# Copied scan states stored as chunk, component, group, together with another order of y rows, outputs and transfers

## The chip, the cores and the metric

The kernel runs on one core of one Trainium2 chip. The metric is the time of one execution on the device, in microseconds, taken over several runs. Five engines work side by side, each through its own instructions in order: TensorE (PE, with its weight loads as PEld), VectorE (DVE), ScalarE (ACT), GpSimd (POOL) and SyncE (SP), which here only issues transfers. A tile scheduler fixes the order in which each engine's instructions stand.

## The reference, cut to what matters

Two sequences (1024 and 512 tokens, 1536 together) go through an attention layer and then through a state-space layer ("S5"). Only the second half of the program, the S5 layer, is changed:

```
u, gate = jnp.split(x @ w_in, 2, axis=-1)
...
bu = einsum('lgp,gnp->lgn', us, b_bar)              # 64 groups, 64 complex states each
_, h = lax.associative_scan(_ssm_combine, (a, bu))  # h[t] = lam * h[t-1] + bu[t], forward and backward
y = einsum('gpn,lgn->lgp', c, h).real + d * uf
y = jax.nn.gelu(y)
y = y * jax.nn.sigmoid(y @ w_glu + b_glu)
return (y * jax.nn.silu(gate)) @ w_out
```

## The kernel before, in words

Tokens are taken in chunks of eight: the 1536 tokens are 192 chunks, 128 of the long sequence and 64 of the short one. What a chunk does within itself is one product with a table `tt`; what it gets from earlier chunks comes through the states at the chunk borders. The scan over those border states runs on VectorE (`step`, L1242 to L1249). It has two halves of 32 groups each, `X[0]` (zone SA) and `X[1]` (zone SB), each stored as chunk, component (real or imaginary), group: 192 x 2 x 32 numbers in a partition, so that two chunks of one group lie 64 numbers apart. Partitions 0 to 63 hold the forward states, 64 to 127 the backward ones, whose chunks run the other way.

Sixteen output steps follow, `i` = 0 to 15, four groups each. `load_s(i)` (L1360) fetches three tiles over SP: `uc` (inputs), `tt` and `wo`. `states_out(i)` (L1371) copies the four groups of `X` into a small tile `st`, turned round in time for the backward half: three copies on ScalarE, L1375, L1376 and L1377, of 1536, 1024 and 512 numbers a partition. `outputs(i, st)` (L1380) makes for each group three products into one PSUM bank: `tt` with `uc` (L1391) and the two components of `wo` with `st` (L1392, L1393). Weights stay in the array; `uc` and `st` are the operands that stream through it, 192 columns each. These products are plain f32, and each is two MATMUL instructions in the trace. ScalarE applies Gelu (L1395), and after every second step eight transfers write a row block `Y[m]` of y to memory (L1399).

The first `N0` = 10 output steps are woven into the last gate passes. A gate pass (`gate`, L1338) multiplies x with the gate weights, which come through six slots of zone R (`load_wg`, L1324); each `mm3` there is three fp32r products (L89, L90, L91) of 512 columns. `between` says behind which of the 48 gate steps of the last six passes an output step stands. `advance` emits scan steps by a running account of microseconds.

After the gate passes comes the GLU: `load_y(m)` brings `Y[m]` back (1536 numbers a partition) and splits it into a rounded part and a rest, on GpSimd for m below 4 (L1440, L1442); `load_w(m)` brings 1/8 of `w_glu` in two halves (L1452) and splits them on ScalarE (L1453) and VectorE (L1454). The raw halves of `load_w(1)` lie in memory that x held (zone X1), so that they can be loaded only when the gate products are done with x. Six output steps, 10 to 15, are woven with the first GLU products (`early`). What is behind that, the rest of the GLU and the output projection, is the same in both kernels.

Of the kernel before, what the change touches and what calls it, by code (L numbers as in the profile page):

```python
# [20 lines left out]
NT = LP + LS  # L21
# [1168 lines left out]
def s5(k):  # L1190
# [59 lines left out]

    owed = [0.0]

# [5 lines left out]
    def advance(us):  # L1258


        owed[0] += us
        while owed[0] > 0 and any(todo.values()):
            steps = [(*h, todo[h].pop(0)) for h in todo if todo[h]]
            owed[0] -= 0.47 * len(steps) if len(steps) > 1 else 0.72
            if len(steps) == 1:
                steps = [(*steps[0], 0, 16), (*steps[0], 16, 32)]
            for f in zip(*[step(*x) for x in steps]):
                for g in f:
                    g()

# [56 lines left out]

    M0, N0 = 2, 10
    passes = [(m, (0, 1, 2)) for m in range(M0)] + [(m, (0,)) for m in range(M0, 8)] + [(m, (1, 2)) for m in range(M0, 8)]
# [8 lines left out]
    def gate(i):  # L1338
        m, cs = passes[i]
        acc = {c: ps_b() for c in cs}  # L1340
        for kt in range(8):
            if i < 2 and kt % 2 == 0:
                states_in(8 + 4 * i + kt // 2)
            if (i, kt) == (1, 6):
                begin(1)
            wg = w.pop((i, kt))
            for c in cs:
                mm3(nc, acc[c], (wg[:, 0, :], wg[:, 1, :]), xk(c, kt), kt == 0, kt == 7)
            fetch()
            advance(0.69 * len(cs) + (1.8 if i < 2 else 0))  # L1350
            if i >= 8 and (i - 8) * 8 + kt in between:
                between.pop((i - 8) * 8 + kt)()
        for c in cs:
            sg = k.rr.tile([128, 512], F32, "sg", 9, 11)
            nc.scalar.copy(sg, acc[c])
            nc.scalar.dma_start(k.SG2[m, :, c * 512:(c + 1) * 512], sg)
# [3 lines left out]
    def load_s(i):  # L1360
        reg, at = ((xa, 0), (xa, 16), (xb, 0))[i % 2 if i < N0 else (i - N0) % 3]
        tag = "%s%d" % ("b" if reg is xb else "a", at)
# [8 lines left out]
    def states_out(i):  # L1371
        reg, at = ((k.xn, 0), (xa, 25))[i % 2]
        st = reg.tile([128, 2, 4, 192], F32, "st", at)
        xv = X[i // 8][:, :, :, (i % 8) * 4:(i % 8) * 4 + 4].rearrange("p c r g -> p r g c")
        nc.scalar.copy(st[0:64], xv[0:64])  # L1375
        nc.scalar.copy(st[64:128, :, :, 0:128], xv[64:128, :, :, 127::-1])  # L1376
        nc.scalar.copy(st[64:128, :, :, 128:192], xv[64:128, :, :, 191:127:-1])  # L1377
        return st

    def outputs(i, st):  # L1380
# [31 lines left out]
    def first(i):  # L1412
        if i == 8:
            advance(1e3)
        outputs(i, states_out(i))
        advance(1.3)
        load(i + 2)

    n = (8 - M0) * 8
    between = {0: lambda: load(0), 3: lambda: load(1)}  # L1420
    for i in range(N0):
        between[6 + (n - 7) * i // max(N0 - 1, 1)] = lambda i=i: first(i)
    for i in range(8, 8 + 8 - M0):
# [4 lines left out]
    xb, xc = Region(k, "X1", (24, F32), (8, F32R)), Region(k, "X2", (32, F32R))  # L1428
    sy = Region(k, "SA", (48, F32R))
    yat = {m: (sy, 12 * m) for m in range(4)}  # L1430
    yat.update({4: (xc, 0), 5: (xc, 12)})
    gat = [(xc, 24), (xb, 24)]
    ys = [None] * 8

    def load_y(m):
        reg, at = yat[m]
        y = reg.tile([128, 2, NT], F32R, "y%d" % m, at)
        raw = bits(y[:, 1])
        nc.sync.dma_start(raw, k.Y[m])
        nc.gpsimd.tensor_scalar(y[:, 0], raw, 1.0, 0.0, op0=ALU.mult, op1=ALU.add)  # L1440

        (nc.gpsimd if m < 4 else nc.vector).tensor_sub(y[:, 1], raw, y[:, 0])  # L1442
        ys[m] = y

    def load_w(m):
        reg, at = gat[m % 3]
        w = reg.tile([128, 2, 8, 128], F32R, "glu", at)
        for h in range(2):
            reg, at = (xb, 22 if m < 3 else (16, 12)[m % 2] + 2 * h) if m else (k.xn, 6 + 2 * h)
            raw = reg.tile([128, 4, 128], F32, "graw%d" % at, at)  # L1450
            hs = slice(4 * h, 4 * h + 4)
            nc.sync.dma_start(raw, k.w_glu[m, :, hs])  # L1452
            nc.scalar.copy(w[:, 0, hs], raw)  # L1453
# [25 lines left out]

    load_y(0)  # L1480
    ws = [load_w(0), load_w(1)]
    load_y(1)
    load(N0 + 2)
    st = states_out(N0)
    big = [ps_s(), ps_s()]
    acc = [[big[i][:, 0:512], big[i][:, 512:1024], ps_b()] for i in range(2)]

    def early(kt):
        if 0 < kt < 5 or kt == 6:
            load_y(kt + 1)  # L1490
        for c in (2, 0, 1):
# [4 lines left out]
    for i in range(N0, 16):  # L1496
        cur = st
        if i < 15:
            st = states_out(i + 1)
        outputs(i, cur)  # L1500
        if i < 13:
            load(i + 3)
        while done < (0, 0, 3, 4, 5, 6)[i - N0]:
            early(done)
            done += 1
        if i == 13:
            x0 = Region(k, "X0", (16, F32R))
            yat[6] = (x0, 0)
            load_y(6)
    while done < 6:  # L1510
# [4 lines left out]
    so = Region(k, "SB", (48, F32R))  # L1515
    gat.append((so, 40))
    early(6)
    ws.append(load_w(2))
    part = [ps_b(), ps_b()]
# [168 lines left out]
```

## Time and profile before

| what | us |
|---|---|
| runs of the kernel before (3) | 1617.59, 1629.79, 1630.28 |
| their median | 1629.79 |
| the profiled execution | 1624.55 |
| its span from first to last instruction | 1622.8 |
| TensorE busy in the span | 1565.0 |
| mean granted TensorE clock | 0.991 |

The profiled execution is 5.2 us under the median and 7 us over the fastest run. Its 1.75 us outside the span are not touched by the change. "Busy" of TensorE counts a matmul from its start to the modelled end of its results, so that two matmuls that follow each other closely overlap; what one costs in a stream is the distance from start to start.

### The profile page before, as it was taken

The numbers are of one execution on the slowest core, as the hardware profiler recorded it, in microseconds if no ns is written. First come the engines' busy times: TensorE is split into PE (matmuls) and PEld (weight loads), VectorE is DVE, ScalarE is ACT, GpSimd is POOL, SyncE is SP. The second block draws the span as 40 slices with busy tenths as digits, with TensorE's granted clock in tenths as the row PEclk, the third lists the DMA queues.
The fourth block names the chain that finished last, engine by engine and source line by source line (L and its number), as shares of the span: only waits on it lengthen the run. The fifth ranks groups of instructions, "written<-read, shape, count | busy, mean of one in ns | idle before, by whom it ended". The sixth has DMA issues, their size and how long they took to land.

```text
span 1622.8 us, 23654 instructions
## 1 busy us (share of the span) xinstructions
PE 1565.0 (96%) x7948; PEld 1324.9 (82%) x7948; DVE 1104.4 (68%) x3077; ACT 633.2 (39%) x1056; POOL 322.7 (20%) x532
## 2 busy tenths in 40 slices
PE   8999999999999999999999999999899889999997
PEld 7997878788888788888888888888678768888886
DVE  5559992767676766888677742499599812565866
ACT  3544331444544445444410113416657367442000
POOL 6820000422223222343201000000000311233110
PEclk9999999999999999999999999999999989999999
DMA  5656566523122325533444427525678857565543
GB/s 194 186 157 207 165 234 219 161 78 92 56 84 86 115 87 182 181 98 103 156 132 127 131 74 192 155 46 157 205 234 245 272 148 229 189 212 162 178 139 88
DMA packets 205929, 249.67 MB, mean 154 GB/s; under 512 B 26608, under 2 KB 149104, under 8 KB 204784
## 3 DMA queue, kind: packets, MB, share of 16 engines
q1 hardware_dynamic: 197168, 232.36, 47.7%
q10 hardware_dynamic: 8640, 15.80, 2.6%
q8 instruction: 63, 1.03, 0.3%
q14 instruction: 58, 0.48, 0.1%
HBM read 155.89 MB, written 90.11 MB: 152 GB/s over the span
## 4 chain that ended last, share of the span: by engine, by line
PE 67%; DVE 12%; DMA 10%; ACT 5%; issue 2%; SPq 2%; POOL 1%; ACTq 0%; DVEq 0%; POOLq 0%
PE B L90 10%; PE B L89 10%; PE B L91 10%; PE S L89 8%; PE S L91 8%; PE S L90 8%; PE B L552 3%; DVE SA L1249 2%; DVE scan L1248 2%; PE S L1229 2%; PE S L518 2%; PE S L517 2%; DMA X<-SG 1%; DMA SA<-CH 1%; DMA X<-in_s_w_out 1%
## 5 line engine op out<-in xcount | busy, mean ns | idle before, releaser
L89 PE MATMUL B<-X,SB 128*128 128x512 f32 x392 | 155.3, 396 | 0.0
L90 PE MATMUL B<-X,SB 128*128 128x512 f32 x392 | 154.0, 393 | 0.0
L91 PE MATMUL B<-X,SB 128*128 128x512 f32 x392 | 153.9, 393 | 0.0
L537 POOL TENSOR_SCALAR SC<-SC,R 128x1024 f32<-128x1024 f32 (+1 forms) x96 | 99.7, 1039 | 209.9 <-DVE R L536 187.1
L554 ACT CAST X<-B 128x512 fp32r<-128x512 f32 x160 | 89.5, 591 | 128.3 <-PE B L552 127.7
L555 DVE TENSOR_TENSOR X<-B,X 128x512 fp32r<-128x512 f32 x160 | 105.7, 682 | 25.5 <-ACT X L554 25.2
L530 ACT ACTIVATE SC<-S,R 128x1024 f32<-128x1024 f32 (+1 forms) x96 | 93.9, 978 | 63.1 <-DVE R L527 58.2
L527 DVE TENSOR_REDUCE R<-S 128x1 f32<-128x1024 f32 (+1 forms) x96 | 99.1, 1038 | 21.9 <-PE S L518 21.6
L552 PE MATMUL B<-ident,SC 128*128 128x128 f32 x640 | 88.7, 272 | 2.0 <-POOL SC L537 2.0
L89 PE MATMUL B<-X,R 128*128 128x512 f32 x192 | 79.2, 413 | 10.7 <-DMA R<-WG 7.3
L552 PEld LDWEIGHTS B<-ident,SC 128*128 128x128 f32 x640 | 76.2, 140 | 16.2 <-POOL SC L537 2.7
L91 PEld LDWEIGHTS B<-X,SB 128*128 128x128 f32 x392 | 74.1, 189 | 15.3
L90 PEld LDWEIGHTS B<-X,SB 128*128 128x128 f32 x392 | 74.1, 189 | 14.7
L89 PEld LDWEIGHTS B<-X,SB 128*128 128x128 f32 x392 | 73.9, 189 | 14.6
L1249 DVE TENSOR_TENSOR SB<-SB,scan 128x32 f32<-128x32 f32 (+1 forms) x504 | 80.8, 213 | 0.5 <-DMA R<-WG 0.5
L1248 DVE TENSOR_TENSOR scan<-SB,lam 128x64 f32<-128x64 f32 (+1 forms) x252 | 64.9, 293 | 17.4 <-ACT SB L1237 17.4
L89 PE MATMUL S<-SA,X 128*128 128x384 f32 (+2 forms) x208 | 70.8, 345 | 5.9 <-POOL SA L96 5.4
L90 PE MATMUL B<-X,R 128*128 128x512 f32 x192 | 76.1, 396 | 0.0
L91 PE MATMUL B<-X,R 128*128 128x512 f32 x192 | 75.8, 395 | 0.0
L1249 DVE TENSOR_TENSOR SA<-SA,scan 128x32 f32<-128x32 f32 (+1 forms) x504 | 75.4, 200 | 0.0
L90 PE MATMUL S<-SA,X 128*128 128x384 f32 (+2 forms) x208 | 70.6, 341 | 0.4 <-DVE SA L97 0.4
L91 PE MATMUL S<-SA,X 128*128 128x384 f32 (+2 forms) x208 | 70.1, 339 | 0.4 <-DVE X L1454 0.4
(454 smaller groups left out, 4230.8 us busy)
## 6 DMA issues: line engine op xcount, KB each, us to landing
R<-WG SPq DMA_DIRECT2D x112, 128.0 KB, 3.5
R<-EU SPq DMA_DIRECT2D x52, 224.0 KB, 3.4
EU<-SA SPq DMA_DIRECT2D x16, 512.0 KB, 3.6
WO<-SA SPq DMA_DIRECT2D x8, 1024.0 KB, 5.3
WG<-X SPq DMA_DIRECT2D x16, 512.0 KB, 3.0
X<-WO SPq DMA_DIRECT2D x16, 512.0 KB, 5.9
SG<-SC ACTq DMA_DIRECT2D x24, 256.0 KB, 3.0
SC<-SG SPq DMA_DIRECT2D x24, 256.0 KB, 2.9
```

The costliest lines, as they stand in the source:

```text
L89: nc.tensor.matmul(ps, ah, bh, start=first, stop=False)
L90: nc.tensor.matmul(ps, ah, bl, start=False, stop=False)
L91: nc.tensor.matmul(ps, al, bh, start=False, stop=last)
L517: nc.tensor.matmul(S[:, cs], qs[:, q], self.kr[kc][0], start=False, stop=False)
L527: nc.vector.reduce_max(nm, self.S[:, :L], axis=AX.X, negate=True)
L530: nc.scalar.activation(P, self.S[:, :L], AF.Exp, bias=nm, accum_out=rsum)
L537: nc.gpsimd.tensor_scalar(P, P, rsum, 0.0, op0=ALU.mult, op1=ALU.add)
L552: nc.tensor.transpose(ps[:, t, :], P[:, (t0 + t) * 128:(t0 + t + 1) * 128], self.k.ident)
L554: nc.scalar.copy(a[:, :, qsl], ps)
L555: nc.vector.tensor_sub(b[:, :, qsl], ps, a[:, :, qsl])
L1248: return [lambda: nc.vector.tensor_mul(t, prev.unsqueeze(2).broadcast_to(sh), lam), lambda: nc.vector.tensor_add(cur, cur, t[:, 0]), lambd ...
L1249: lambda: nc.vector.tensor_add(cur, cur, t[:, 0]), lambda: nc.vector.tensor_add(cur, cur, t[:, 1])]
```

## The change

The code changes in five places.

- `states_out` stores `st` as chunk, component, group (192 x 2 x 4). A copy now reads and writes in the same order, in runs of four numbers, and the products L1398 and L1399 (L1392 and L1393 before) read `st` with a step of eight numbers from column to column. For steps 8 to 15 the forward copy goes to VectorE, held behind the scan's last instruction.
- `N0` is 8: eight output steps stand among the gate passes, and eight (half 1 of the scan) are woven with the GLU.
- The y rows 0 to 2 are fetched while the gate passes still run (`rows`), their rounding goes to ScalarE (`hi_y`) and the rest to VectorE behind the scan (`lo_y`); GpSimd keeps the rounding of rows 4 to 7.
- The slots and the order of the transfers of `load_s` change for the last steps, and some y and `w_glu` transfers are kept where they are written.
- The gate results of the first two passes lie in the zone of `st` instead of zone R.

```diff
-    M0, N0 = 2, 10
+    M0, N0 = 2, 8
...
-            sg = k.rr.tile([128, 512], F32, "sg", 9, 11)
+            sg = k.xn.tile([128, 512], F32, "sg", 0, 2, 4, 6) if i < 2 else k.rr.tile([128, 512], F32, "sg", 9, 11)
...
-        st = reg.tile([128, 2, 4, 192], F32, "st", at)
-        xv = X[i // 8][:, :, :, (i % 8) * 4:(i % 8) * 4 + 4].rearrange("p c r g -> p r g c")
-        nc.scalar.copy(st[0:64], xv[0:64])
-        nc.scalar.copy(st[64:128, :, :, 0:128], xv[64:128, :, :, 127::-1])
-        nc.scalar.copy(st[64:128, :, :, 128:192], xv[64:128, :, :, 191:127:-1])
+        st = reg.tile([128, 192, 2, 4], F32, "st", at)
+        xv = X[i // 8][:, :, :, (i % 8) * 4:(i % 8) * 4 + 4]
+        if i < N0:
+            nc.scalar.copy(st[0:64], xv[0:64])
+        else:
+            with k.tc.issue_after(last[0].ins):
+                nc.vector.tensor_copy(st[0:64], xv[0:64])
+        nc.scalar.copy(st[64:128, 0:128], xv[64:128, 127::-1])
+        nc.scalar.copy(st[64:128, 128:192], xv[64:128, 191:127:-1])
...
-                nc.tensor.matmul(o, wo[:, 0, g, :], st[:, 0, g, :], start=False, stop=False)
-                nc.tensor.matmul(o, wo[:, 1, g, :], st[:, 1, g, :], start=False, stop=True)
+                nc.tensor.matmul(o, wo[:, 0, g, :], st[:, :, 0, g], start=False, stop=False)
+                nc.tensor.matmul(o, wo[:, 1, g, :], st[:, :, 1, g], start=False, stop=True)
...
+    def fetch_y(m):
+        reg, at = yat[m]
+        ys[m] = reg.tile([128, 2, NT], F32R, "y%d" % m, at)
+        pin(nc.sync.dma_start(bits(ys[m][:, 1]), k.Y[m]))
+
+    def hi_y(m):
+
+        y = ys[m]
+        if m < 4:
+            pin(nc.scalar.copy(y[:, 0], bits(y[:, 1])))
+        else:
+            nc.gpsimd.tensor_scalar(y[:, 0], bits(y[:, 1]), 1.0, 0.0, op0=ALU.mult, op1=ALU.add)
+
+    def lo_y(m):
+        with k.tc.issue_after(last[0].ins):
+            nc.vector.tensor_sub(ys[m][:, 1], bits(ys[m][:, 1]), ys[m][:, 0])
...
-        between[6 + (n - 7) * i // max(N0 - 1, 1)] = lambda i=i: first(i)
+        between[6 + (n - 12) * i // (N0 - 1)] = lambda i=i: first(i)
+    between[n - 5] = rows
+    between[n - 1] = lambda: [hi_y(m) for m in range(3)]
...
-    load_y(0)
-    ws = [load_w(0), load_w(1)]
-    load_y(1)
+    st = states_out(N0)
+    ws = [load_w(0)]
     load(N0 + 2)
-    st = states_out(N0)
+    ws.append(load_w(1))
+    fetch_y(3)
...
+        if i < 11:
+            lo_y(i - 8)
+        elif i == 11:
+            hi_y(3)
+            lo_y(3)
+        elif i in (12, 14):
+            load_y(i // 2 - 2)
         outputs(i, cur)
-        if i < 13:
-            load(i + 3)
-        while done < (0, 0, 3, 4, 5, 6)[i - N0]:
+        for x in ((), (11,), (12, 13), (14,), (15,), (), (), ())[i - N0]:
+            load(x)
+        while done < (0, 0, 1, 2, 3, 3, 4, 4)[i - N0]:
             early(done)
             done += 1
```

TensorE at the end of the gate passes. The last gate products write a bank `B` from x (`X_91`) and zone R; the GLU products write the double bank `S` from y rows (`SA`) and the split `w_glu` of block 0 (`X_11904`, after `X_11864`) or 1 (after `X_11863`). Before:

```order
L91 MATMUL B<-X_91,R 128x512
L1391 MATMUL B<-X_10777 128x192 x2
L89 MATMUL S<-SA,X_11904 128x512
L90 MATMUL S<-SA,X_11904 128x512
L91 MATMUL S<-SA,X_11904 128x512
```

After:

```order
L91 MATMUL B<-X_91,R 128x512
L1397 MATMUL B<-X_10776 128x192 x2
L1397 MATMUL B<-X_10777 128x192 x2
L89 MATMUL S<-SA,X_11864 128x512
L89 MATMUL S<-SA,X_11863 128x512
L90 MATMUL S<-SA,X_11864 128x512
L91 MATMUL S<-SA,X_11864 128x512
L90 MATMUL S<-SA,X_11863 128x512
```

Before, 48 GLU products follow here and then the output steps 10 onward; after, 14 of them stand ahead of output step 8, and the third already needs the rest part of y row 0.

VectorE at the end of the scan (L1248 and L1249 on `SB`), with the split of the two halves of `load_w(1)` (`X_11903`, after `X_11863`). Before, the rest parts of y rows 0 to 3 are not in this list, since GpSimd makes them:

```order
L1249 TENSOR_TENSOR SB<-SB,scan_81 128x2x16 x3
L1454 TENSOR_TENSOR X_11903<-X_11902,X_11903 128x512
L1249 TENSOR_TENSOR SB<-SB,scan_81 128x2x16
L1248 TENSOR_TENSOR scan_81<-SB,lam 128x4x16 x2
L1249 TENSOR_TENSOR SB<-SB,scan_81 128x2x16 x4
L1442 TENSOR_TENSOR X_11904<-X_11904 128x1536
```

After, 18 scan instructions stand behind the second half, then the rest of y row 0 and the forward copies of steps 8 and 9:

```order
L1249 TENSOR_TENSOR SB<-SB,scan_81 128x2x16 x4
L1478 TENSOR_TENSOR X_11863<-X_11862,X_11863 128x512
L1248 TENSOR_TENSOR scan_81<-SB,lam 128x4x16 x2
L1249 TENSOR_TENSOR SB<-SB,scan_81 128x2x16 x4
L1248 TENSOR_TENSOR scan_81<-SB,lam 128x4x16 x2
L1249 TENSOR_TENSOR SB<-SB,scan_81 128x2x16 x4
L1248 TENSOR_TENSOR scan_81<-SB,lam 128x4x16 x2
L1249 TENSOR_TENSOR SB<-SB,scan_81 128x2x16 x4
L1442 TENSOR_TENSOR SA<-SA 128x1536
L1381 COPY XN<-SB 64x1536
L1381 COPY X_10777<-SB 64x1536
```

The end of the scan, and with it everything on VectorE behind it, stands in both kernels behind the split of `load_w(1)`.

SyncE at the same place, before (`X_11902` is the raw slot of `w_glu`, and the tiles of an output step where it reads EU, CH, WO):

```order
L1399 DMA Y<-X_10776 16x8x192 x8
L1324 DMA R<-WG 128x256 x4
L1439 DMA SA<-Y 128x1536
L1452 DMA X_11902<-in_w_glu 128x512
L1364 DMA X_11902<-EU 128x4x192
```

After:

```order
L1325 DMA R<-WG 128x256 x5
L1366 DMA X_10777<-EU 128x4x192
L1368 DMA X_10777<-CH 128x512
L1370 DMA X_10777<-WO 128x2x512
L1405 DMA Y<-X_10776 16x8x192 x8
L1366 DMA X_11862<-EU 128x4x192
L1368 DMA X_11862<-CH 128x512
L1370 DMA X_11862<-WO 128x2x512
L1476 DMA X_11862<-in_w_glu 128x512 x3
```

The last gate weights now go ahead of the eight y writes, and the first half of `load_w(1)` goes behind the three tiles of an output step instead of ahead of them.

## Rows read from the trace of the kernel before

**Rows 1.** The page, part 1: busy us, share, instructions of each engine.
```profile
PE 1565.0 (96%) x7948; PEld 1324.9 (82%) x7948; DVE 1104.4 (68%) x3077; ACT 633.2 (39%) x1056; POOL 322.7 (20%) x532
```

**Rows 2.** Busy time by stretch: length, engines' busy us, granted clock, DMA share, GB/s.
```profile
1165.00:1280.00 115.00, 111.58 (x531) 93.25 (x530) 115.00 (x829) 66.79 (x57) 2.81 (x2) 1.00 0.80 249
1280.00:1305.00 25.00, 18.64 (x72) 13.80 (x71) 15.61 (x20) 4.60 (x8) 17.03 (x7) 0.93 0.78 239
1305.00:1350.00 45.00, 35.74 (x157) 32.58 (x157) 6.88 (x39) 35.88 (x25) 1.47 (x1) 0.85 0.61 188
```

**Rows 3.** What TensorE waited for from 1280 to 1385: total, times, longest.
```profile
PE B L89 <- DMA R<-WG: 5.3, 2, 3.1
PE B L1392 <- ACT XN L1377: 4.8, 2, 2.5
PE B L1392 <- ACT XN L1376: 3.6, 1, 3.6
```

**Rows 4.** TensorE in order of time at output step 13: start, us, instruction.
```profile
1353.80 0.49 PE L1392 MATMUL B<-X,X 128*128 128x192 f32 x2
1354.13 0.49 PE L1393 MATMUL B<-X,X 128*128 128x192 f32 x2
1354.45 0.49 PE L1391 MATMUL B<-X 128*128 128x192 f32 x2
```

**Rows 5.** ScalarE's groups with shapes apart: busy us, mean ns, idle before.
```profile
L1376 ACT COPY XN<-SA 64x1024 f32<-64x1024 f32 x4 | 8.1, 2037 | 0.0
...
L1376 ACT COPY XN<-SB 64x1024 f32<-64x1024 f32 x4 | 7.7, 1930 | 0.1
...
L682 ACT CAST SB<-X 128x1024 fp32r<-128x1024 f32 x6 | 6.3, 1054 | 11.4 <-DMA X<-in_s_w_out 11.4
L1453 ACT CAST X<-X 128x512 fp32r<-128x512 f32 x10 | 6.1, 614 | 18.3 <-DMA X<-in_w_glu 17.1 <-PE S L90 1.1
...
L1377 ACT COPY XN<-SA 64x512 f32<-64x512 f32 x4 | 4.3, 1086 | 0.0
L1377 ACT COPY XN<-SB 64x512 f32<-64x512 f32 x4 | 4.3, 1071 | 0.0
```

**Rows 6.** TensorE in order of time, 1278 to 1350 (idle before in brackets).
```profile
1284.54 0.50 PE L89 MATMUL B<-X,R 128*128 128x512 f32 x1 [2.22 <-DMA R<-WG]
...
1293.38 0.80 PE L89 MATMUL B<-X,R 128*128 128x512 f32 x1 [3.11 <-DMA R<-WG]
1293.98 0.63 PE L90 MATMUL B<-X,R 128*128 128x512 f32 x1
1294.40 0.63 PE L91 MATMUL B<-X,R 128*128 128x512 f32 x1
...
1300.25 0.39 PE L91 MATMUL B<-X,R 128*128 128x512 f32 x1
...
1304.58 0.39 PE L89 MATMUL S<-SA,X 128*128 128x512 f32 x1
1304.81 0.39 PE L90 MATMUL S<-SA,X 128*128 128x512 f32 x1
```

**Rows 7.** VectorE in order of time, end of the scan.
```profile
1311.65 0.69 DVE L1454 TENSOR_TENSOR X<-X,X 128x512 fp32r<-128x512 f32 x1 [3.04 <-ACT X L1453]
...
1312.36 0.35 DVE L1248 TENSOR_TENSOR scan<-SB,lam 128x64 f32<-128x64 f32 x2
1312.63 0.54 DVE L1249 TENSOR_TENSOR SB<-SB,scan 128x32 f32<-128x32 f32 x4
1347.88 1.76 DVE L1442 TENSOR_TENSOR X<-X 128x1536 fp32r<-128x1536 f32 x1 [34.72 <-POOL X L1440]
```

**Rows 8.** SyncE's issues in order of time, around the last gate product.
```profile
1282.93 6.38 SPq L1399 DMA_DIRECT2D Y<-X  x8
...
1299.99 0.33 SPq L1452 DMA_DIRECT2D X<-in_w_glu  x1
...
1301.96 10.73 SPq L1452 DMA_DIRECT2D X<-in_w_glu  x3
```

More of the change, by code (lines that the diff above doesn't have):

```diff
@@ L1249, in step @@
                 lambda: nc.vector.tensor_add(cur, cur, t[:, 0]), lambda: nc.vector.tensor_add(cur, cur, t[:, 1])]
-    owed = [0.0]
+    owed, last = [0.0], [None]
+    pin = k.tc.keep_in_program_order
     def begin(half):
@@ L1268, in advance @@
                 for g in f:
-                    g()
+                    last[0] = g()
     def load_u(m):
@@ L1360, in load_s @@
     def load_s(i):
-        reg, at = ((xa, 0), (xa, 16), (xb, 0))[i % 2 if i < N0 else (i - N0) % 3]
+        reg, at = ((xa, 0), (xa, 16), (xb, 0))[i % 2 if i < N0 else (0, 1, 2, 1, 2, 0, 1, 2)[i - N0]]
         tag = "%s%d" % ("b" if reg is xb else "a", at)
@@ L1412, in first @@
     def first(i):
-        if i == 8:
-            advance(1e3)
         outputs(i, states_out(i))
@@ L1420, in s5, with load_y, rows @@
     between = {0: lambda: load(0), 3: lambda: load(1)}
+    yat, ys = {}, [None] * 8
+    def fetch_y(m):
[11 more added lines that the diff above has]
+            nc.vector.tensor_sub(ys[m][:, 1], bits(ys[m][:, 1]), ys[m][:, 0])
+    def load_y(m):
+        fetch_y(m)
+        hi_y(m)
+        lo_y(m)
+    def rows():
+        sy = Region(k, "SA", (48, F32R))
+        yat.update({m: (sy, 12 * m) for m in range(4)})
+        for m in range(3):
+            fetch_y(m)
     for i in range(N0):
-        between[6 + (n - 7) * i // max(N0 - 1, 1)] = lambda i=i: first(i)
+        between[6 + (n - 12) * i // (N0 - 1)] = lambda i=i: first(i)
+    between[n - 5] = rows
+    between[n - 1] = lambda: [hi_y(m) for m in range(3)]
     for i in range(8, 8 + 8 - M0):
@@ L1428, in s5 @@
     xb, xc = Region(k, "X1", (24, F32), (8, F32R)), Region(k, "X2", (32, F32R))
-    sy = Region(k, "SA", (48, F32R))
-    yat = {m: (sy, 12 * m) for m in range(4)}
     yat.update({4: (xc, 0), 5: (xc, 12)})
     gat = [(xc, 24), (xb, 24)]
[L1433 to L1443, printed above, removed]
     def load_w(m):
@@ L1451, in load_w @@
             hs = slice(4 * h, 4 * h + 4)
-            nc.sync.dma_start(raw, k.w_glu[m, :, hs])
+            (pin if m == 1 else lambda x: x)(nc.sync.dma_start(raw, k.w_glu[m, :, hs]))
             nc.scalar.copy(w[:, 0, hs], raw)
@@ L1488, in early @@
     def early(kt):
-        if 0 < kt < 5 or kt == 6:
-            load_y(kt + 1)
         for c in (2, 0, 1):
@@ L1508, in s5 @@
             yat[6] = (x0, 0)
-            load_y(6)
+    load_y(6)
     while done < 6:
@@ L1516, in s5 @@
     gat.append((so, 40))
+    ws.append(load_w(2))
+    load_y(7)
     early(6)
-    ws.append(load_w(2))
     part = [ps_b(), ps_b()]
```

## The prediction

> **What bounds the kernel now.** I read the busy times of the engines first. TensorE is busy for 1565.0 of 1622.8 us, and no other engine for more than 68% [rows 1]. So a change counts by what it does to the length of TensorE's own stream, and by the few places where TensorE waits. Next I read the busy times by stretch, to find these places in the part that is changed. While the scan runs (1165 to 1280) TensorE is busy for 111.6 of 115 us although VectorE has no free moment, so there is little to gain there. From 1280 to 1305 TensorE is idle for 6.4 of 25 us, and from 1305 to 1350 for 9.3 of 45 us with a granted clock of 0.85 [rows 2]. Two places, then: the last gate products, and the GLU products and output steps behind them.
>
> The list of waits gives the causes. At the gate products it is two arrivals of gate weights, 5.3 us together; at the output steps it is ScalarE's copies into `st`, 4.8 and 3.6 us [rows 3]. SyncE's list shows why the weights are late: eight y writes take 6.38 us of the queue from 1282.93 on [rows 8], and the four weight transfers stand behind them in the order shown above. TensorE waits in that time, until 1293.38 [rows 6].
>
> **The change part by part.** *The products with `st`.* There are 16 steps of four groups with two such products, 128 in all, each of two MATMUL instructions, so 256 with 192 columns each. At output step 13 two products in a row take from 1353.80 to 1354.45, so 0.325 us a product, 162.5 ns a MATMUL and 0.85 ns a column [rows 4]. The change makes each column's number stand 32 bytes behind the last one. No TensorE instruction of the kernel before reads an operand with a step, so the trace has no price for it. It has ScalarE's, by the slopes between two lengths, which leave out the fixed cost. With adjacent numbers: (1054 - 614)/512 = 0.86 ns a number (L682, L1453). With the step of 64 numbers of the old copies: (2037 - 1086)/512 = 1.86 ns from SA, (1930 - 1071)/512 = 1.68 ns from SB [rows 5]. TensorE's 0.85 ns is nearly the pace of the first, so I take the second for the stepped read, 1.68 to 1.86, in the middle 1.77 ns. A MATMUL then takes 192 x 1.77 = 340 ns, 177 ns more, and 256 of them 45.4 us more; by the ends 41.0 and 49.7 us. TensorE hides nothing of this, since the products stand in its own stream. The bounds are wider. Below, the price can be nothing: the step is read by another engine here, and TensorE's own path may be quicker. A gain is excluded, as the same columns pass through the same array. Above, if each f32 MATMUL passes over its columns twice and each time pays 1.77 ns, it is 680 ns, 517 more, and the sum +132 us.
>
> [...]
>
> *The copies into `st`.* They go from a step on one side to runs of four on both. I expect them to fall from 1.7 to 1.9 ns towards 0.86 ns a number [rows 5], and half of them to leave ScalarE for VectorE from step 8 on. VectorE has the room, 6.9 busy of 45 us [rows 2]. ScalarE is not the bound, so this is worth no more than the waits it ends, below.
>
> *The end of the gate passes.* The five last weight transfers now stand ahead of the y writes, and GpSimd's rounding of y rows no longer stands in this stretch. The two waits for weights, 5.3 us [rows 3], should go, and with them the cold clock that follows the second: from 1293.98 to 1294.40 a product takes 0.42 us where it is 0.23 us later (1304.58 to 1304.81) [rows 6], over seven products 1.4 us. For shorter copies ahead of the woven output steps I allow another 0.8 us. Sum: 7.5 us less.
>
> *Behind the gate passes.* Here a wait is added. Before, TensorE had GLU products to do from the last gate product (1300.25, done at about 1300.6 [rows 6]) to about 1311, and only then met the copies. After, the third GLU product needs the rest part of y row 0, which VectorE makes behind the last scan instruction, and the scan's end stands in both kernels behind the split of the second half of `load_w(1)`. In the trace that split begins at 1311.65 and the scan ends at 1313.17 (1312.63 and 0.54 us) [rows 7]; the first of its transfers is issued at 1299.99 [rows 8]. With the rest part of 1.76 us [rows 7] TensorE would go on at about 1315, 14.4 us after the last gate product, and it has some 1.8 us to do in between: eight f32 MATMULs and two GLU products. In addition 18 scan instructions stand behind that split instead of 6; the six take 0.81 us (1312.36 to 1313.17), so that is 1.6 us more. That makes 14.2 us idle, and 1 to 2 us of cold clock behind it. What it replaces: 9.3 us idle from 1305 to 1350, about 1.0 us of the idle time from 1300.6 to 1305 (6.36 less the 5.3 of the weights), and a clock of 0.85 over 35.7 busy us, which costs 5.4 us [rows 2]. That is 15.7 us against some 15.7, so nothing is left of it either way; I keep 6 us to each side. To the worse side lies that the first half of `load_w(1)` now stands behind three tiles of an output step, 128 x 2304 numbers or 1.18 MB, which at the 188 GB/s of that stretch [rows 2] is 6.3 us. To the better side lies that the waits for copies may end outside the stretch counted too. VectorE's queue behind the waiting split holds the rest of the scan, the rest parts and the forward copies, so all of them move together.
>
> *The others* cost nothing: the gate results of two passes in another zone (four of ScalarE's copies, same length), and the rounding of y rows 0 to 2 on ScalarE, three instructions of about 1.5 us (1054 ns and 512 x 0.86 [rows 5]) that hide behind the scan's end, for which TensorE waits anyway.
>
> *Sum:* 1624.55 + 45.4 - 7.5 + 0 = 1662.4, so **1662 us**, made against the profiled execution, which lies 5.2 us under the median of 1629.8. With the ends of the price and 6 us to either side it is 1652 to 1673, and I give 1648 to 1676 as the likeliest case's own range.
>
> **The rivals.** *The step is free.* Then the time is 1624.55 - 7.5 = 1617, or 1606 to 1626 with what the stretch behind the gate passes may give or take: not slower than before. For it speaks that an fp32r product takes a column in 0.23/512 = 0.45 ns [rows 6], so the f32 stream, with 0.85, may leave every second read unused, and a read of half the pace would be hidden. Against it speaks that the two readers of different kinds, at 0.86 and 0.85 ns, stand equally close to the pace at which ScalarE did pay for a step. The point from which it decides: 7.5 us over 256 MATMULs are 29 ns each, so at 192 columns the change gains below 1.0 ns a column, and loses above.
>
> *The columns are read twice.* 1624.55 + 132 - 7.5 = 1749 us. For it speaks the same 0.45 ns: 0.85 may be two passes at that pace. Against it, that if each pass merely fell to half its pace the sum would be the forecast's again.
>
> *The wait behind the gate passes is longer.* The price of the step as forecast and the 6.3 us for the three tiles on top: 1669 us. For it speaks that the tiles stand ahead in the queue; against it, that SyncE issues the transfers within 2 us of each other (1299.99 to 1301.96 [rows 8]) and that they share the same engines anyway.
>
> *The change doesn't do what it says.* If runs of four are copied no faster, ScalarE still gives half of each step to VectorE, and some of the waits for copies return: up to 8.4 us [rows 3] on top of whichever case holds.
>
> **How the numbers follow.** The forecast (a price near 1.77 ns, 1662 us) has a chance of 0.51, the free step 0.33, the two reads 0.10, the longer wait 0.06. A difference of 1%, 16 us, is about what a measurement of this kernel tells from no change; against 1629.8 the bounds are 1613.5 and 1646. The free step gives faster in half of its cases and no change in the other half. The forecast gives slower but for 0.04, where the price is part of what I took. So faster 0.17, same 0.20, slower 0.63. Both signs hold much of this, so the range must reach to the free step: 1611 to 1688 leaves out the two reads, a third of the free step's lower half and the edges of the forecast, about 0.2.
>
> **What would show it right or wrong.** In the changed kernel's trace, the step from one product with `st` to the next at L1398 and L1399: 0.68 us if I am right, 0.325 if the step is free, over 1.2 if it is read twice. The product with `uc` (L1397) stays at 0.325. ScalarE's copies of 1024 and 512 numbers near 1.05 and 0.6 us. No wait for gate weights of more than 1 us around the y writes. One wait of about 14 us on VectorE's L1442 right behind the last gate product, and no large wait on the copies after it. I am wrong if the price of the step lies outside 1.4 to 2.1 ns a column, or if that wait is under 8 or over 20 us.

## The result, and the profile after

The changed kernel takes 1662.85 us (median of 6 runs, 1660.77 to 1666.07); the kernel before, with runs beside these, 1626.13 us (6 runs). The ratio is 1.024, with an interval of 1.0216 to 1.0263. The forecast was 1662 us. The profiled execution of the changed kernel took 1666.07 us, its span 1664.3 us, 41.5 us more than the span of before.

The busy times of the engines, as in [rows 1]:

```profile
PE 1607.3 (97%) x7948; PEld 1336.2 (80%) x7948; DVE 1104.6 (66%) x3089; ACT 581.5 (35%) x1052; POOL 303.0 (18%) x524
```

TensorE has the same 7948 instructions and is busy 42.3 us longer. ScalarE lost 51.7 us of work, and the time still went up. TensorE in order of time at output step 14 of the changed kernel shows where TensorE's part comes from; [rows 4] are the same instructions before:

```profile
1384.87 0.85 PE L1398 MATMUL B<-X,X 128*128 128x192 f32 x2
1385.54 0.87 PE L1399 MATMUL B<-X,X 128*128 128x192 f32 x2
1386.23 0.51 PE L1397 MATMUL B<-X 128*128 128x192 f32 x2
1386.58 0.85 PE L1398 MATMUL B<-X,X 128*128 128x192 f32 x2
```

From start to start the two products with `st` take 0.67 and 0.69 us, and the product with `uc` behind them 0.35. A group of three takes 1.71 us (1384.87 to 1386.58) where it took 0.975 before, so 64 groups cost 47 us. A MATMUL with the step takes 340 ns, 1.77 ns a column.

ScalarE's groups with shapes apart, the answer to [rows 5]:

```profile
L1378 ACT COPY XN<-SA 64x1536 f32<-64x1536 f32 x4 | 5.9, 1478 | 0.5 <-DVE scan L1248 0.4
...
L1382 ACT COPY XN<-SB 64x1024 f32<-64x1024 f32 x4 | 4.2, 1044 | 2.9 <-DVE SB L1249 2.8
...
L1383 ACT COPY XN<-SB 64x512 f32<-64x512 f32 x4 | 2.4, 612 | 0.0
```

The copies of 1024 and 512 numbers fell from 1930 and 1071 ns to 1044 and 612: 0.84 ns a number. What TensorE waited for from 1150 to 1440, as in [rows 3]:

```profile
PE S L90 <- DVE SA L1442: 7.7, 1, 7.7
PE S L89 <- ACT X L1477: 7.0, 1, 7.0
PE B L89 <- DMA R<-WG: 2.8, 7, 0.7
```

The long waits for gate weights and those for the copies are gone. Instead there are two new ones. TensorE in order of time at the end of the gate passes, where [rows 6] stood before:

```profile
1318.41 0.39 PE L91 MATMUL B<-X,R 128*128 128x512 f32 x1
1318.64 1.14 PE L1397 MATMUL B<-X 128*128 128x192 f32 x6
1320.01 0.59 PE L1397 MATMUL B<-X 128*128 128x192 f32 x2 [0.23 <-ACT R L1357]
1320.65 0.50 PE L89 MATMUL S<-SA,X 128*128 128x512 f32 x1
1328.14 0.79 PE L89 MATMUL S<-SA,X 128*128 128x512 f32 x1 [6.99 <-ACT X L1477]
1336.61 0.80 PE L90 MATMUL S<-SA,X 128*128 128x512 f32 x1 [7.68 <-DVE SA L1442]
```

And VectorE in the same stretch, the answer to [rows 7]:

```profile
1320.63 0.69 DVE L1478 TENSOR_TENSOR X<-XN,X 128x512 fp32r<-128x512 f32 x1 [38.65 <-ACT X L1477]
...
1328.12 0.69 DVE L1478 TENSOR_TENSOR X<-X,X 128x512 fp32r<-128x512 f32 x1 [3.83 <-ACT X L1477]
...
1332.03 0.69 DVE L1478 TENSOR_TENSOR X<-X,X 128x512 fp32r<-128x512 f32 x1 [0.82 <-ACT X L1477]
...
1334.36 0.53 DVE L1249 TENSOR_TENSOR SB<-SB,scan 128x32 f32<-128x32 f32 x4
1334.80 1.75 DVE L1442 TENSOR_TENSOR SA<-SA 128x1536 fp32r<-128x1536 f32 x1
```

The number to look at is the 38.65. VectorE had almost finished the scan at 1282 and then stood still, because the next instruction in its queue was the split of a `w_glu` half. Pieces of the scan's end stand behind each of the splits, and the rest part of y row 0, for which TensorE waits, stands behind all of it. ScalarE in order of time shows what the splits themselves waited for:

```profile
1319.37 0.58 ACT L1357 COPY R<-B 128x512 f32<-128x512 f32 x1 [0.63 <-DMA Y<-X]
1319.98 0.62 ACT L1477 CAST X<-XN 128x512 fp32r<-128x512 f32 x1
...
1327.47 0.62 ACT L1477 CAST X<-X 128x512 fp32r<-128x512 f32 x1 [6.35 <-DMA X<-in_w_glu]
1331.38 0.62 ACT L1477 CAST X<-X 128x512 fp32r<-128x512 f32 x1 [3.29 <-DMA X<-in_w_glu]
```

The split at 1320.63 is the first of `load_w(0)`. That block's transfers were issued at 784.8 and 1156.7, so the 38.65 us are not a wait for a transfer: the cast ahead of the split stands in ScalarE's queue right behind the copy of the last gate result (L1357), at the end of the gate passes. The two halves of `load_w(1)` do wait for their transfers, one after the other, since both use the same raw slot: the first is issued at 1320.10, and the second only at 1328.84, when the first has been split.

The span can be divided at two points of TensorE's stream: the first product with `uc` and the last gate product. In the kernel before, too, the products with `st` of steps 8 and 9 start behind the last gate product, although `N0` is 10: 128 of the 256 MATMULs with `st` stand on either side of it in both kernels. The middle stretch grew from 98.5 us (1201.7 to 1300.25) to 112.7 (1205.7 to 1318.41), the last one from 322.6 to 345.9. Each holds half of the stepped products, 23.5 us. So the middle stretch gained 9.3 us (0.65 us of it because four MATMULs with `uc` moved behind the last gate product) and the last one nothing (0.2). The 4.0 us ahead of the first product lie before anything that the forecast spoke of; that point lies between 1196 and 1206 in all the profiles below, in no order that fits an edit, and I do not attribute them. Each figure for a stretch, here and below, comes from one profiled execution.

### The profile page after: what moved, and what is told of

Read it like the earlier page. It is cut to its first block, busy times and chain, and to the rows that moved or that the text cites. A ratio compares the mean times of both kernels' runs of the same rounds, so it can differ in the third digit from the quotient of the medians.

```text
span 1664.3 us, 23665 instructions
## 1 busy us (share of the span) xinstructions
PE 1607.3 (97%) x7948; PEld 1336.2 (80%) x7948; DVE 1104.6 (66%) x3089; ACT 581.5 (35%) x1052; POOL 303.0 (18%) x524
## 4 chain that ended last, share of the span: by engine, by line
PE 73%; DVE 13%; DMA 9%; ACT 2%; SPq 1%; issue 1%; POOL 1%; DVEq 0%; ACTq 0%; POOLq 0%
PE B L89 10%; PE B L90 10%; PE B L91 10%; PE S L89 9%; PE S L91 9%; PE S L90 9%; PE B L552 3%; PE B L1399 3%; PE B L1398 3%; DVE SA L1249 3%; PE S L1229 2%; DVE scan L1248 2%; PE S L518 2%; PE S L517 2%; DMA R<-WG 1%
## 5 line engine op out<-in xcount | busy, mean ns | idle before, releaser
L91 PEld LDWEIGHTS B<-X,SB 128*128 128x128 f32 x392 | 74.1, 189 | 15.3
L89 PEld LDWEIGHTS B<-X,SB 128*128 128x128 f32 x392 | 74.1, 189 | 14.7
L89 PE MATMUL S<-SA,X 128*128 128x384 f32 (+2 forms) x208 | 71.9, 352 | 12.7 <-ACT X L1477 7.0
L90 PE MATMUL S<-SA,X 128*128 128x384 f32 (+2 forms) x208 | 72.2, 349 | 8.0 <-DVE SA L1442 7.7
L1249 DVE TENSOR_TENSOR SB<-SB,scan 128x32 f32<-128x32 f32 (+1 forms) x504 | 76.9, 203 | 0.2 <-PE B L91 0.2
L1249 DVE TENSOR_TENSOR SA<-SA,scan 128x32 f32<-128x32 f32 (+1 forms) x504 | 73.6, 200 | 0.0
L91 PE MATMUL S<-SA,X 128*128 128x384 f32 (+2 forms) x208 | 72.1, 347 | 0.0
L1248 DVE TENSOR_TENSOR scan<-SB,lam 128x64 f32<-128x64 f32 (+1 forms) x252 | 54.8, 251 | 22.7 <-ACT SB L1237 22.7
```

Of the source, the lines that this page charges most:

```text
L89: nc.tensor.matmul(ps, ah, bh, start=first, stop=False)
L90: nc.tensor.matmul(ps, ah, bl, start=False, stop=False)
L91: nc.tensor.matmul(ps, al, bh, start=False, stop=last)
L1248: return [lambda: nc.vector.tensor_mul(t, prev.unsqueeze(2).broadcast_to(sh), lam), lambda: nc.vector.tensor_add(cur, cur, t[:, 0]), lambd ...
L1249: lambda: nc.vector.tensor_add(cur, cur, t[:, 0]), lambda: nc.vector.tensor_add(cur, cur, t[:, 1])]
```

## The experiments

Theories at the start. Mine: the step of eight is the whole loss, because TensorE takes longer over a column that is read with a step (0.67 and 0.69 us a product instead of 0.325); the order of the work is worth some 7 us. Its rival: a good part of the loss is the new order with its wait behind the gate passes. Within mine it was open what the price goes by: the same for any step, or by the distance from column to column.

**order_alone.** The changed kernel with the old layout of `st`:

```diff
-        st = reg.tile([128, 192, 2, 4], F32, "st", at)
+        st = reg.tile([128, 2, 4, 192], F32, "st", at)
...
-                nc.tensor.matmul(o, wo[:, 0, g, :], st[:, :, 0, g], start=False, stop=False)
+                nc.tensor.matmul(o, wo[:, 0, g, :], st[:, 0, g, :], start=False, stop=False)
```

> The changed kernel with the old layout of st (component, group, chunk): the products read adjacent numbers, the copies go back to a step of 64 numbers (forward copies of steps 8 to 15 on VectorE). My theory (the step of eight is the whole loss, and the new order is worth 7 to 9 us at the gate products and nothing behind them): a product 0.325 us, and the profiled run 128 x 0.36 = 46 us under the changed kernel's, so 1612 to 1622 us, 0.5% faster than before or no difference that shows; the waits for VectorE's rest of y row 0 and for w_glu behind the gate passes, 14.7 us in the changed kernel, stay. Rival (a good part of the loss lies in the new order, for instance in that wait): 1630 us or more with products at 0.325 us.

Measured: 1618.39 us, ratio 0.9956 (0.9941 to 0.9971). TensorE's waits behind the gate passes (1286 to 1440) are those of the changed kernel:

```profile
PE S L90 <- DVE SA L1442: 7.7, 1, 7.7
PE S L89 <- ACT X L1477: 7.5, 1, 7.5
```

So the layout costs 44.5 us in this order (1662.85 less 1618.39), and the order by itself is a small gain, in spite of its wait of 15.2 us. The rival falls. Between the two division points order_alone takes 95.6 us, only 3.0 less than before, and from 1100 on it still waits 5.7 us for gate weights.

**layout_alone.** The kernel before with the new layout alone:

```diff
-        st = reg.tile([128, 2, 4, 192], F32, "st", at)
-        xv = X[i // 8][:, :, :, (i % 8) * 4:(i % 8) * 4 + 4].rearrange("p c r g -> p r g c")
+        st = reg.tile([128, 192, 2, 4], F32, "st", at)
+        xv = X[i // 8][:, :, :, (i % 8) * 4:(i % 8) * 4 + 4]
...
-                nc.tensor.matmul(o, wo[:, 0, g, :], st[:, 0, g, :], start=False, stop=False)
+                nc.tensor.matmul(o, wo[:, 0, g, :], st[:, :, 0, g], start=False, stop=False)
```

> The kernel before with the new layout of st alone (copies in runs of four, products with a step of eight numbers; order, N0, y rows and transfers as before). My theory: 128 products at 0.68 instead of 0.325 us and the product behind each pair 0.02 us longer, +47 us; against it the waits for the copies (8.4 us) and some of the waits for gate weights (5.3 us) end, because the copies are shorter and the stream ahead of the weights is longer: 1658 to 1670 us. Rival (the order carries part of the loss): under 1650 us.

Measured: 1653.95 us, ratio 1.0171 (1.0139 to 1.0203), 4 us under the lower end that I gave: the loss without the new order is 28 us and not 44.5. The busy times by stretch, from the last gate product to the last output step, of this kernel:

```profile
1320.30:1400.40 80.10, 77.42 (x281) 54.68 (x281) 18.19 (x52) 35.47 (x47) 8.43 (x5) 0.98 0.58 175
```

and of order_alone:

```profile
1292.40:1360.50 68.10, 52.84 (x274) 47.68 (x273) 33.71 (x79) 35.27 (x39) 2.94 (x2) 0.87 0.67 205
```

In the old order with short copies TensorE is idle for 2.7 of 80.1 us, at a clock of 0.98; in the new order with long copies for 15.3 of 68.1 us, at 0.87. Short copies do not end the two waits of the new order (14.7 us in the changed kernel, 7.7 and 7.2 us in step2 below). I had counted the waits for the copies against the 47 us, and not the clock that goes with them. From the last gate product to the end layout_alone takes 9.4 us more than before, although its products cost 23.5 more there. So the short copies and the longer stream together gave back 14 us, and in the changed kernel the new order takes as much again. The run before_step2 below has the short copies without the longer stream.

**step4** and **step2.** The layout changed so that the columns of a product lie four and two numbers apart:

```diff
-        st = reg.tile([128, 192, 2, 4], F32, "st", at)
+        st = reg.tile([128, 2, 192, 4], F32, "st", at).rearrange("p r c g -> p c r g")
```

```diff
-        st = reg.tile([128, 192, 2, 4], F32, "st", at)
-        xv = X[i // 8][:, :, :, (i % 8) * 4:(i % 8) * 4 + 4]
+        st = reg.tile([128, 2, 2, 192, 2], F32, "st", at).rearrange("p r q c g -> p c r q g")
+        xv = X[i // 8][:, :, :, (i % 8) * 4:(i % 8) * 4 + 4].rearrange("p c r (q g) -> p c r q g", q=2)
...
-                nc.tensor.matmul(o, wo[:, 0, g, :], st[:, :, 0, g], start=False, stop=False)
+                nc.tensor.matmul(o, wo[:, 0, g, :], st[:, :, 0, g // 2, g % 2], start=False, stop=False)
```

> The changed kernel with st as component, chunk, group: the products read with a step of four numbers (16 bytes), the copies write and read runs of four as before. [...] Theory C (price by distance): about half of the addition, 0.5 us and 1640 us.

> The changed kernel with st as component, pair of groups, chunk, two: the products read with a step of two numbers (8 bytes), the copies go in runs of two. [...] Theory B (each step other than one costs the same): a product 0.68 us and 1663 us, as the changed kernel. Theory C (the price grows with the bytes from column to column): a product between 0.4 and 0.6 us, 1628 to 1650 us.

Measured: step4 1657.36 us (one run); step2 1619.47 us, ratio 0.9949 (0.9933 to 0.9965), the same as order_alone. TensorE's group of L1399 (mean ns behind the bar) of step4:

```profile
L1399 PE MATMUL B<-XN,X 128*128 128x192 f32 x64 | 27.5, 519 | 0.0
```

and of step2:

```profile
L1399 PE MATMUL B<-XN,X 128*128 128x192 f32 x64 | 16.1, 331 | 0.0
```

With adjacent numbers it is 326, with the step of eight 527. These means run to a MATMUL's modelled end; the price is the distance from start to start, and TensorE in order of time in step2 has it:

```profile
1348.74 0.50 PE L1398 MATMUL B<-X,X 128*128 128x192 f32 x2
1349.08 0.50 PE L1399 MATMUL B<-X,X 128*128 128x192 f32 x2
1349.42 0.49 PE L1397 MATMUL B<-X 128*128 128x192 f32 x2
```

A product takes 0.34 us with the step of two, where it takes 0.325 with adjacent numbers, and 0.67 with the step of four. So four costs nearly what eight does (0.67 us against 0.67 and 0.69), and two costs about 5%. Theories B and C fall for the f32 products: the step of two has neither the price of eight nor a share of it by distance.

**step64.** The products read `X` itself:

```diff
-                nc.tensor.matmul(o, wo[:, 0, g, :], st[:, :, 0, g], start=False, stop=False)
+                nc.tensor.matmul(o, wo[:, 0, g, :], X[i // 8][:, :, 0, (i % 8) * 4 + g], start=False, stop=False)
```

> The changed kernel, but the products L1398 and L1399 read X itself, where the columns of a group lie 64 numbers (256 bytes) apart; the copies into st are still made and not read, so the turn of time for the backward half is left out of the outputs. [...]

Measured: 1647.2 us (one run), and the group of L1399:

```profile
L1399 PE MATMUL B<-SA,X 128*128 128x192 f32 x64 | 26.5, 503 | 0.0
```

A product takes 0.64 us from start to start, a little under the 0.67 of step4. For the f32 products the distance adds nothing from the step of four on (0.67 us with four, 0.67 and 0.69 with eight, 0.64 with 64).

**f32_runs.** `st` as chunk pair, component, group, two, and from step 8 on chunk quad, component, group, four (the copies, changed to match, are left out here):

```diff
-        st = reg.tile([128, 192, 2, 4], F32, "st", at)
+        t = 2 if i < 8 else 4
+        st = reg.tile([128, 192 // t, 2, 4, t], F32, "st", at)
...
-                nc.tensor.matmul(o, wo[:, 0, g, :], st[:, :, 0, g], start=False, stop=False)
+                nc.tensor.matmul(o, wo[:, 0, g, :], st[:, :, 0, g, :], start=False, stop=False)
```

> The changed kernel with st as chunk pair, component, group, two (steps 0 to 7) and chunk quad, component, group, four (steps 8 to 15): the f32 products read runs of two columns 16 numbers apart, and runs of four 32 apart; the copies are two for each one and slower. Theory P: a product takes 0.325 us in both. [...] Theory M: 0.68 us in both. Only the products are compared, since the copies differ.

Measured: 1618.17 us (one run), all products at the old pace; the group of the second product:

```profile
L1403 PE MATMUL B<-XN,X 128*128 128x192 f32 x64 | 15.1, 325 | 0.0
```

Theory M, full pace for an unbroken row only, falls for f32: a product takes 0.325 us from start to start with runs of two and with runs of four, as with an unbroken row; the step of two costs about 5% (0.34 us).

**glu_steps** and **glu_runs.** The same question put to the other type: the fp32r products of the GLU, 512 columns each, with another order of the same columns. Both runs start from order_alone; the second edit is shown against the first.

```diff
+    steps = {3: 2, 4: 4, 5: 8, 6: 16, 7: 64}
...
-        mm3(nc, ps, (w[:, 0, kt], w[:, 1, kt]), (ys[kt][:, 0, cs], ys[kt][:, 1, cs]), kt == 0, kt == 7)
+        s = steps.get(m, 1)
+        hi, lo = (ys[kt][:, j, cs].rearrange("p (a b) -> p b a", b=s) for j in range(2))
+        mm3(nc, ps, (w[:, 0, kt], w[:, 1, kt]), (hi, lo), kt == 0, kt == 7)
```

```diff
-    steps = {3: 2, 4: 4, 5: 8, 6: 16, 7: 64}
+    runs = {3: (2, 8), 4: (2, 64), 5: (4, 16), 6: (8, 32), 7: (1, 3)}
...
+            hi, lo = (v.rearrange("p (a b t) -> p b a t", b=s // t, t=t) if s != 3 else v[:, ::-1] for v in (hi, lo))
```

> The run order_alone with a step put on the streamed operand of other products: the fp32r products of the GLU (L89 to L91, 512 columns, 72 for each of the output blocks 3 to 7) read the same columns of a y row in another order, with a step of 2, 4, 8, 16 and 64 numbers in block 3, 4, 5, 6 and 7; the sigmoid undoes the order when it reads PSUM. Base: 0.227 us a product. [...] Theory B (a step halves the pace of each pass, and an f32 MATMUL is two passes): step 2 stays at 0.227, 4 to 64 take 0.45 us; 64 us more. If the price grew with the distance, 64 would cost more than 4.

> As glu_steps, but the streamed operand goes in runs of adjacent numbers: block 3 in runs of 2 with 8 numbers from run to run, block 4 in runs of 2 with 64, block 5 in runs of 4 with 16, block 6 in runs of 8 with 32, and block 7 backward (step -1). Theory P (adjacent pairs: full pace needs that each number's neighbour in memory is read next to it): 0.227 us in blocks 3 to 6. [...] Theory M (the fp32r products have their full pace for an unbroken row only): 0.43 to 0.49 in all of them. [...]

Measured: 1699.2 and 1650.11 us (one run each). TensorE in order of time in glu_steps, two starts with the step of 2, 4, 8 and 64:

```profile
1419.40 0.63 PE L89 MATMUL B<-SA,X 128*128 128x512 f32 x1
1419.85 0.63 PE L90 MATMUL B<-SA,X 128*128 128x512 f32 x1
...
1455.23 0.64 PE L89 MATMUL B<-X,X 128*128 128x512 f32 x1
1455.70 0.64 PE L90 MATMUL B<-X,X 128*128 128x512 f32 x1
...
1475.00 0.61 PE L89 MATMUL B<-SA,SB 128*128 128x512 f32 x1
1475.43 0.61 PE L90 MATMUL B<-SA,SB 128*128 128x512 f32 x1
...
1530.40 0.67 PE L89 MATMUL B<-X,X 128*128 128x512 f32 x1
1530.89 0.67 PE L90 MATMUL B<-X,X 128*128 128x512 f32 x1
```

and in glu_runs, with runs of 2 (eight numbers from run to run) and runs of 4:

```profile
1410.70 0.64 PE L91 MATMUL B<-X 128*128 128x512 f32 x1
1411.16 0.64 PE L89 MATMUL B<-X,X 128*128 128x512 f32 x1
...
1461.89 0.38 PE L91 MATMUL B<-SA,SB 128*128 128x512 f32 x1
1462.11 0.38 PE L89 MATMUL B<-SA,SB 128*128 128x512 f32 x1
```

The distance from one start to the next is the price: 0.45, 0.47, 0.43 and 0.49 us for the steps, 0.43 also for 16; 0.46 for runs of 2 with eight numbers from run to run and 0.49 with 64; 0.22 for runs of 4. Runs of 8 and the backward row took 0.22 and 0.23. So an fp32r column costs 0.43 to 0.46 ns where four or more adjacent numbers are read one behind the other, and 0.84 to 0.95 ns in the other patterns measured. Theory B of glu_steps did not hold: it has the steps of 4 to 64 right (0.43 to 0.49 us against its 0.45) and the step of two wrong (0.45 against its 0.227). In glu_runs P and M fall, the first by the runs of two, the second by the runs of four. The two types differ: runs of two are free in f32 (0.325 us a product) and the step of two nearly so (0.34), while in fp32r both take twice the time (0.45 to 0.49 us instead of 0.227).

**before_step2.** The kernel before, with the layout of step2 and nothing else (same edit as above).

> The kernel before, with st as component, pair of groups, chunk, two (step of two numbers for the products, runs of two for the copies) and nothing else. Theory: what the order of the kernel before lost behind its gate products was the long copies, so it ends here without a price on TensorE: the run layout_alone less 46 us, 1604 to 1612 us, 1% or more faster than before, and TensorE idle behind the gate passes 3 us instead of 11. Rival: the waits come back, since the stream is 46 us shorter: over 1616 us.

Measured: 1618.61 us, ratio 0.9952 (0.9932 to 0.9972); the rival was right. Behind the last gate product it is 9.8 us better than before (303.8 against 313.6 us up to TensorE's last start), where I had expected 14: some 4 us of what layout_alone gave back there came with its longer stream. Ahead of it the waits for gate weights stand as before: 5.6 us in two waits. Between the two division points it takes 100.1 us against 98.5 before.

**step2_free, step2_late, step2_queues.** Three edits, each on top of the one before it, on the wait behind the gate passes:

```diff
+            if m < 2:
+                with k.tc.issue_after(last[0].ins):
+                    nc.vector.tensor_sub(w[:, 1, hs], raw, w[:, 0, hs])
```

```diff
-                glu(acc[i][c], ws[i], kt, c)
+                if kt == 0:
+                    with k.tc.issue_after(mm[9].ins):
+                        glu(acc[i][c], ws[i], kt, c)
```

```diff
-                with k.tc.issue_after(last[0].ins):
+                with k.tc.issue_after(cp[8 + m, 0].ins):
+                    nc.scalar.copy(w[:, 0, hs], raw)
+                with k.tc.issue_after(cp[8 + m, 1].ins):
                     nc.vector.tensor_sub(w[:, 1, hs], raw, w[:, 0, hs])
...
-    st = states_out(N0)
+    st, st9 = states_out(N0), states_out(N0 + 1)
```

> The run step2 with one edit: the rest parts of the first two w_glu blocks (VectorE) are held behind the last scan instruction, so that the end of the scan no longer stands in VectorE's queue behind a split that waits for its transfer. Theory (the 14.9 us of idle TensorE behind the gate passes are that queue): the forward copies and the rest parts of y rows come before w_glu, TensorE goes on with output steps 8 and 9 during the wait, and idle behind the gate passes falls from 15 to under 7 us; 1608 to 1614 us. Rival (the transfers of w_glu set the end in any order): idle stays over 12 us and the time at 1617 to 1621 us.

> The run step2_free with one edit: the first row of GLU products (kt = 0) is held behind the last product of output step 9 on TensorE. In step2_free TensorE still waits 6.8 us for the first half of w_glu block 1 right behind the gate passes, with steps 8 and 9 queued behind it. Theory: these 28 products of 0.33 us, some 8 us of work, fill that wait; idle behind the gate passes falls from 8 to 1 to 3 us and the time by 4 to 6 us, to 1603 to 1606 us. Rival (steps 8 and 9 have operands of their own that are late, or the GLU then waits as long): the time stays within 2 us of 1609.

> The run step2_late with the same thing done on ScalarE and VectorE: the two parts of w_glu blocks 0 and 1 are made behind the copies of the states of steps 8 and 9, so that these copies no longer queue behind a cast that waits for its transfer (in step2_late the cast stood until 1299.00 and the copy came at 1299.65, while the scan had been done at about 1282.8). Theory: the copies and the rest parts of the y rows come before the last gate product is done, TensorE goes on with steps 8 and 9 at once, and idle behind the gate passes falls from 10.8 to under 4 us; with the clock that the wait costs, 6 to 10 us less than step2_late, 1597 to 1602 us. Rival (the 9.8 us are the transfers' and only move to the w_glu products): idle stays over 8 us and the time within 2 us of 1607.5.

Measured: 1609.28 us (ratio 0.990, 0.987 to 0.9931), 1607.5 (0.991, 0.9884 to 0.9936) and 1603.76 (0.9874, 0.9854 to 0.9893). The first edit ended the wait for VectorE's rest part, as expected; 6.8 us of wait for the cast of the first half of `load_w(1)` stayed. The second did nothing that can be told, as its rival had it: the wait changed its name. ScalarE in order of time in step2_late shows why:

```profile
1299.00 0.62 ACT L1477 CAST X<-X 128x512 fp32r<-128x512 f32 x1 [7.44 <-DMA X<-in_w_glu]
1299.65 1.10 ACT L1382 COPY XN<-SB 64x1024 f32<-64x1024 f32 x1
```

The copy of the states, whose scan had ended at 1282.8, stood in the queue behind a cast that waited for its transfer. With the third edit TensorE's waits from 1286 to 1440 are

```profile
PE B L1397 <- ACT X L1401: 1.1, 1, 1.1
PE B L1398 <- ACT XN L1382: 0.9, 1, 0.9
PE B L1397 <- ACT R L1357: 0.6, 1, 0.6
PE B L89 <- ACT X L1501: 0.2, 1, 0.2
```

and the mean clock of the execution is 0.998. Idle behind the gate passes fell from 10.8 to 2.8 us, and the time by 3.7 (medians) to 8.7 us (profiled executions), so by the medians less than the 6 to 10 us expected. This is the fastest version, 1.3% under the kernel before and 3.6% under the changed one.

## Why the prediction was right

**The price of the step.** Forecast 45.4 us (41.0 to 49.7); measured 47 us in the stream (64 groups, 0.735 us each), 44.5 us between order_alone and the changed kernel. The value of 1.77 ns a column was met. What it was taken from was less sure than it looked: I had only ScalarE's slope to go by, and TensorE's agrees in size, but not in kind. In ScalarE the price came with the old copies' step of 64; for TensorE the runs show that a step is not dear in itself. With two numbers a product takes 0.34 us instead of 0.325, with four 0.67. That the step of this change was one of the dear ones, and that ScalarE's price for another step had TensorE's size, was luck. One rule for both types does not come out of the runs: the f32 products keep nearly their full pace with two (the mean of a MATMUL is 331 ns in step2 and 519 ns in step4), while the fp32r products take 0.46 and 0.49 us with runs of two and have their full pace, 0.22 and 0.23 us, with runs of four and eight and backward. What sets the price is not shown.

**The free step**, the rival of 0.33, supposed an idle half of the f32 stream (an estimate from 0.85 against 0.45 ns a column). The step of two, nearly free in f32 and twice the time in fp32r, fits such a slack; that it is the reason is not shown. Steps of four and more are not hidden (0.64 to 0.69 us an f32 product instead of 0.325). **The two reads** (0.10) are out for the f32 products at the price it had, 1749 us. Whether an f32 MATMUL passes over its columns twice stays open: fp32r at 0.84 to 0.95 ns for a step of four or more is half of the f32 price of 1.67 to 1.77, which would fit two passes, but the step of two and the runs of two do not (0.885 and 0.90 to 0.95 ns in fp32r, 0.85 to 0.89 in f32).

**The end of the gate passes.** Forecast -7.5 us, measured -9.3. The size was near, the reason was half wrong. I gave the gain to the new order of the transfers; but order_alone has only 3.0 us of it and still waits 5.7 us for weights. With short copies as well (step2, 92.0 us between the division points) it is 6.5, and with the step of eight on top the 9.3. In the old order short copies alone gain nothing (before_step2, 100.1 us), and with the step of eight 7.3 us come (layout_alone, 114.7 us against 98.5 + 23.5). So in either order a part comes only with the longer stream. That the weights then have the time to arrive fits the waits for them, 1.7 us in layout_alone against 7.0 in before_step2 from 1195 on, and is not shown beyond that.

**Behind the gate passes.** Forecast: 14.2 us of new idle time, in place of as much; measured 14.7 us in two waits, and a sum of 0.2 us. The two halves are shown apart: in the old order short copies give 14 us back with the longer stream (layout_alone) and 9.8 without it (before_step2); the new order takes them (order_alone has 15.2 us of waits). I had named one wait of about 14 us, on VectorE's L1442; that one took 7.7 us, under the 8 that I had set as a sign of being wrong, and there is a second one of 7.0 us ahead of it, on ScalarE's cast of the first half of `load_w(1)`. So the end of the wait was right, and its course was not: I had counted both GLU products ahead of the rest part as free to go, and the second of them needs that half. I had also not seen that the scan is held from 1282 on, 38 us, already by the splits of `load_w(0)`.

**The copies** fell as expected (1.05 and 0.6 us), and their waits went. **The wait longer by 6.3 us** (0.06) did not come: the split of the second half began 13.6 us after the last gate product (1318.41 to 1332.03), before 11.4 (1300.25 to 1311.65), 2.2 us more in all. Yet the first half did come later: its cast began 7.4 us after the issue (1320.10 to 1327.47), where it took 2.7 before (1299.99 to 1302.68), and the second half won 3.4 of these back (2.5 us against 5.9). My argument against this rival, two issues within 2 us, misread the row: the second half is issued at 1305.13, after the first has been split. A raw slot for each half was not tried.

**The sum.** Part of the closeness of 1662 to 1662.85 is luck too. Between the two profiled executions, against which the sum was made, the difference is 41.5 us and not 37.9: the products with `uc` cost 1.6 us that I had not counted, the stretch ahead of the first of them 4.0 us, and the gate passes gained 1.8 us more than forecast. The product with `uc` did not stay at 0.325, as I had said, but took 0.35 us.

## What to carry to other kernels

Before a layout is turned round to make a copy cheap, price the other reader: an operand that streams through TensorE is read once for every product, here on the engine that sets the end (busy for 97% of the span), and a copy on an engine with slack (ScalarE, busy for 39% before) cost here only the waits that it set: before_step2, with short copies, is 0.5% faster than the kernel before. Between the two layouts there was a third here: pairs (step of two, 8 bytes) give the copy nearly all of its gain (1.10 and 1.12 us for 1024 numbers in step2_late, against 1.93 and 1.97 before and 1.04 in the changed kernel) and leave the f32 products within 5% of their pace.

When a wait ends and the time does not fall, look in the queues for work that was ready long before and stands behind an instruction that is itself held up. The scan's end stood for 38 us on VectorE behind a split whose cast came only at the end of the gate passes, and in step2_late the copies stood on ScalarE behind a cast that waited for its transfer. Taking out the first brought 10 us (step2 to step2_free), and only when the second was out too did the wait behind the gate passes fall under 3 us.

## What was not expected of the hardware

- TensorE's streamed operand, from start to start: an f32 column costs 0.85 ns adjacent or in runs of 2 or 4, 0.89 with a step of 2, 1.74 with 4, 1.77 with 8, 1.67 with 64. An fp32r column costs 0.43 to 0.46 ns adjacent, backward or in runs of 4 or 8, and 0.84 to 0.95 in runs of 2 and with the steps of 2, 4, 8, 16 and 64.
- The product with `uc` behind two stepped ones takes 0.35 us instead of 0.325.
- VectorE copied 64 x 1536 f32 numbers in 0.95 us in runs of four (0.62 ns each, the changed kernel), in 0.96 and 0.97 us in runs of two (step2_late) and in 1.53 us with a step of 64 numbers on the source (order_alone): the factor there is 1.6, on ScalarE it is 2.0 (1480 ns in the changed kernel and 2995 before).
